# One kernel, three stretches re-ordered: explicit orders in the first mixer, a routing table stored in two parts, and attention woven into the delta recurrence

## The chip, the cores and the metric

The kernel runs on one core of a Trainium2 chip. The number that counts is the device time of one execution in microseconds (us); smaller is better. The core has a matrix engine (TensorE, PE in the profile), a vector engine (DVE), a scalar engine (ACT), a general engine (POOL, used here for indirect loads) and a queue that issues transfers (SP). Each engine executes its own instructions in the order in which they were written for it, and waits at the first one whose inputs are not there.

## The reference

Two layers over 512 tokens of width 1024, in fp32. The first is a mixer (a convolution branch and a linear recurrence) and a layer of 16,384 experts of which each token uses 8 x 16; the second is a hybrid of attention and a gated delta rule.

```
ada = silu(c) @ w_ada + b_ada          # six groups: sh1 sc1 g1 sh2 sc2 g2
z = modulate(rmsnorm(x), sh1, sc1) @ w_in
y_a = gate_b * conv3(gate_c * xa)
y_b = rg_lru(conv4(xr)) * gelu(gr)     # sigmoid gates, exp, sqrt, scan
y = concat(head_rmsnorm(y_a), head_rmsnorm(y_b)) @ w_out
x = x + g1 * y
h = modulate(rmsnorm(x), sh2, sc2)
q = h @ w_q ; sc = q . sub_keys ; top 16 x 16 -> best 16 per head -> softmax g
x = x + g2 * sum_k g_k * gelu(h . U[idx_k]) * V[idx_k]
...
proj = rms_norm(x) @ w_in2             # a_q a_k a_v a_z  d_q d_k d_v d_z  d_b d_a
attn = softmax(a_q a_k^T/8 - slope*dist, causal) @ a_v * silu(a_z)     # 8 heads of 64
o = gated_delta_rule(silu(conv(d_q, d_k, d_v)), g, beta)               # 4 heads of 128, 8 chunks of 64
out = rms_norm(x + rms_norm(concat(attn, rms_norm(o) * silu(d_z)) @ w_out2))
```

With 512 tokens the block selection of the attention takes every earlier block, so it is plain causal attention.

## The kernel before

Activations lie feature-major: 128 partitions by 512 tokens, eight such tiles for the width. An exact fp32 product is made of three fp32r matmuls: `_split` (lines 98 to 103) makes a high part on ACT (line 101: `wH`, `hidH`, `yH`, `cH`, `vH`) and the rest on DVE (line 102: `wL`, `yL`, `vL`), and `_mm3` (lines 106 to 110) adds high x high, high x low and low x high in one PSUM bank. The list scheduler of the framework decides in which order each engine gets the instructions; `tc.issue_after` adds an edge to that order, and the `weave` calls with the numbers of `PLAN` say how generators of work are dealt out against each other.

Five stretches follow one another:

- **First mixer.** `ada(s, dc)` multiplies a 128 x 1024 block of `w_ada` with the broadcast vector `cb` and sums it (line 218, `wada`, DVE). `rms_row` squares (line 265), adds, sums over partitions by tiny matmuls (`ps_ts`), takes the root (line 163 on ACT) and the reciprocal (line 164 on DVE), and spreads it by `ps_row`. Then `xn` (line 298), `hidH` (line 301), and eight steps `dc` of `w_in` into the banks `zp`, `np`, `gp`. The branches end in `headnorm` (lines 386 to 397), and `w_out` runs in two halves of four output tiles on the four `zp` banks, which the update of `xT` on DVE (line 432) releases.
- **Scores, routing, spread.** Top 16 of the scores on DVE (lines 455 to 459), and a dense gate table: one-hot tiles `ohA`, `ohB` (fp16) are multiplied into `ps_g`, 128 x 128 for each token. ACT copies four tokens at a time into `st`, 128 x (128 keys x 32 tokens), and each full `st` (2 MB) goes to `gd` in DRAM (lines 663 and 665).
- **Expert loop.** For each of the 128 first keys `c`: `S = h . U` for 128 experts (`psS`), gelu into `ring`, times the gates `g` read back from `gd` (lines 733 and 741), split into `cH`, `cL`, and `pv` adds `V[c]` (lines 749 to 755).
- **Second mixer.** `proj(m)` is a product of 24 matmuls of 512 columns. `delta_inputs`, `heads` and `recurrence` are the delta rule: inverses of 128 x 128 blocks (`ps_inv`, line 952), transposes (`ps_tm`), then a chain of four steps `ps_w`, `vn`, `ps_s`, `S` (lines 1075 to 1085). `attention(j)` (line 1104) handles two heads of 64 features: the first head's `ps_l` (line 1130, 64 partitions deep) with its softmax, its four value products `ps_ao` (line 1154, 64 columns of weights), and then the second head.
- **Output projection.** `ps_m`, 384 matmuls of 256 columns, whose first bank set is `ps`, `ps`, `ps`, `po`, and the last norms.

Of the kernel before, what the change touches and what calls it, by code (L numbers as in the profile page):

```python
# [20 lines left out]
P = 128  # L21
# [9 lines left out]
GN = 4  # L31
LAG = 46
# [81 lines left out]
PLAN = [(18, 8), (18, 60), (12, 24)]  # L114
# [3 lines left out]
class _Weights:  # L118
# [6 lines left out]
    def get(self):  # L125
        k = self.k
        while self.srcs and len(self.raw) < 2:
            self.load()
        while self.raw and len(self.parts) < 2:
            self.split()  # L130
        return self.parts.pop(0)

# [89 lines left out]
def _phase1(k):  # L222

    nc, tc, I = k.nc, k.tc, k.I
    with tc.tile_pool(name="p1", bufs=1, reuse_waits="tile") as p1, \
# [11 lines left out]
        nc.scalar.activation(out=c1, in_=c1, func=AF.Silu)  # L237
        root = p1.tile([P, 1], F32, name="root")
        nc.scalar.activation(out=root, in_=k.eps, func=AF.Sqrt)
# [22 lines left out]
        def add_square(dc):  # L262
# [4 lines left out]
            if dc:  # L267
                nc.vector.tensor_tensor(out=sqs[0], in0=sqs[0], in1=sq, op=OP.add)

        def rms_row():  # L270

            r = tile_("rms", "rms", 2, (P, 4))
            _rstd(k, r, _token_sums(k, pps, [[sqs[0]]], "np", 2), 1.0 / D)
            sqs.clear()
            return _row_by_transposes(k, pps, lambda tb: r[:, tb:tb + 1].broadcast_to([P, P]), "np", 2)

        for dc in range(KC):
            add_square(dc)
# [5 lines left out]
        rps = rms_row()  # L284
# [5 lines left out]
        for dc in range(KC):  # L290
            sc, sh = ada(1, dc), ada(0, dc)
            nc.vector.tensor_tensor(out=sh, in0=sh, in1=k.col("b_ada", dc, 1), op=OP.add)
            A = A1[:, dc:dc + 1]
            nc.vector.scalar_tensor_tensor(out=A, in0=sc, scalar=k.col("norm1_g", dc, 1), in1=G1[:, dc:dc + 1],
                                           op0=OP.mult, op1=OP.add)
            t = tile_("xn", ("gate0", "gate1")[dc // 4], 4)
            with tc.issue_after(mod.ins) if dc else ExitStack():
                nc.vector.scalar_tensor_tensor(out=t, in0=xT[:, dc, :], scalar=A, in1=row if dc else rps,
                                               op0=OP.mult, op1=OP.mult)
            with tc.issue_after(k.weights.last.ins) if dc else ExitStack():  # L300
                nc.scalar.activation(out=hH[:, dc, :], in_=t, func=AF.Identity, bias=sh)
# [6 lines left out]
        with tc.issue_after(mod.ins):  # L308
            kc_ = _softplus(k, p1, k.neglam, 4, "lru_k")
# [70 lines left out]
        def headnorm(ys, gname, m0):  # L380
# [11 lines left out]
            for j, y in enumerate(ys):  # L392
# [4 lines left out]
                nc.vector.scalar_tensor_tensor(out=y, in0=y, scalar=k.col(gname, j, 1), in1=row,  # L397
                                               op0=OP.mult, op1=OP.mult)
# [17 lines left out]
        g1, sh2, sc2 = (ada_group(s, k.conv_end) for s in (2, 3, 4))  # L416
# [3 lines left out]
        for m in range(KC):  # L420
# [110 lines left out]
def _peer(k, psum):  # L531
# [10 lines left out]
    gd = k.dr.tile([NG, P, NK, GT], F32, name="gd")  # L542
# [25 lines left out]
    with ExitStack() as bctx:  # L568
# [63 lines left out]
        def spread(b, iT, gHL):  # L632
# [11 lines left out]
            for gq in range(P // GT):  # L644
                st = po.tile([P, NK, GT], F32, name="st", tag="st", bufs=2)
                for to in range(0, GT, OG):
# [9 lines left out]
                    for j0 in range(0, OG, 4):  # L656
# [138 lines left out]
def _mixer2(k, psum, pv):  # L795
# [138 lines left out]
    for tb in range(4):  # L934
        for hf in range(2):
# [3 lines left out]
            o = tile_("x3", "lg", 5)  # L939
# [164 lines left out]
    def attention(j):  # L1104
# [13 lines left out]
        nc.scalar.activation(out=az, in_=az, func=AF.Silu)  # L1118
        yield
        po = pps.tile([P, T], F32, name="ps_ao", tag="po", bufs=1)  # L1120
        for hh in range(2):
            h = 2 * j + hh
            off = hh * 64
            rows = slice(off, off + 64)
            slope = 2.0 ** -(h + 1)
            pr = []
            for qb in range(4):
                nk = (qb + 1) * P
# [3 lines left out]
                lg = tile_("lg", "lg", 5)  # L1132
                nc.vector.scalar_tensor_tensor(out=lg[:, 0:nk], in0=C["alibi"][:, 384 - qb * P:512], scalar=slope,
                                               in1=ps[:, 0:nk], op0=OP.mult, op1=OP.add)
                mx = p4.tile([P, 2], F32, name="mx", tag="mx", bufs=6)
                nc.vector.tensor_reduce(out=mx[:, 0:1], in_=lg[:, 0:nk], axis=AX.X, op=OP.max)
                nc.vector.tensor_scalar(out=mx[:, 0:1], in0=mx[:, 0:1], scalar1=-1.0, scalar2=None, op0=OP.mult)
                nc.scalar.activation(out=lg[:, 0:nk], in_=lg[:, 0:nk], func=AF.Exp, bias=mx[:, 0:1],
                                     accum_out=mx[:, 1:2])
                nc.vector.reciprocal(out=mx[:, 1:2], in_=mx[:, 1:2])  # L1140
                nc.vector.tensor_scalar(out=lg[:, 0:nk], in0=lg[:, 0:nk], scalar1=mx[:, 1:2], scalar2=None, op0=OP.mult)
                pr.append(lg)
                yield
            for kb in range(4):
                nq = (4 - kb) * P
                ps = pps.tile([P, T], F32, name="ps_pT", tag="pa", bufs=2)
                for qb in range(kb, 4):
                    nc.tensor.transpose(ps[:, (qb - kb) * P:(qb - kb + 1) * P], pr[qb][:, kb * P:(kb + 1) * P], k.ident)
                pT = tile_("pT", "pT", 3)
                if kb % 2:  # L1150
# [3 lines left out]
                nc.tensor.matmul(out=po[rows, kb * P:T], lhsT=av[:, kb, off:off + 64], rhs=pT[:, 0:nq],  # L1154
                                 start=kb == 0, stop=kb == 3)
                yield
        nc.vector.tensor_tensor(out=az, in0=az, in1=po, op=OP.mult)
        azs.append(az)

# [51 lines left out]
    for _ in A:  # L1211
        pass
    G = chain(gates_of_delta(), gated_norm())
    weave(B, 200, G, 10)
    for _ in G:
        pass
    for az in azs:
        ya = k.px.tile([P, 2, T], F32R, name="ya", tag="row", bufs=4)
        _split(k, az, ya[:, 0, :], ya[:, 1, :])
        yv.append((ya[:, 0, :], ya[:, 1, :]))  # L1220
    yH, yL = k.new_hid()
    for m, y in enumerate(yd):
# [22 lines left out]
    for q in range(4):  # L1245
        acc = [bank("m", tag) for tag in (("ps", "ps", "ps", "po"), ("pp", "pp", "pa", "pa"))[q % 2]]
# [154 lines left out]
```

## Time and profile before

| | before |
|---|---|
| median of 3 runs | 1864.59 us (1864.06 to 1872.85) |
| profiled execution | 1863.24 us, of which span 1861.5 us |
| busy in the span | PE 1777.6 us (95%), DVE 1480.4 (80%), ACT 831.2 (45%), POOL 333.7 (18%) |
| granted TensorE clock, mean | 0.984 |
| first mixer | 0 to 216 us |
| scores, routing, spread | 216 to 566 us |
| expert loop | 566 to 1430 us |
| second mixer, output | 1430 to 1861.5 us |

A span is the time from the first instruction to the last; 1.74 us of the profiled time lie outside it. The shares are means over stretches with different limits, so a stretch has to be read by itself.

### The profile page before, as it was taken

Reading aid. Unit: us, or ns where it says so; the run is one execution under the profiler, and the core shown is the slowest. Engines: PE = TensorE matmul, PEld = TensorE weight load, DVE = VectorE, ACT = ScalarE, POOL = GpSimd, SP = SyncE. Lnnn points to the kernel's source line nnn. Section 1 sums busy time; section 2 is a strip of 40 time slices with the busy share of each in tenths; the row PEclk is TensorE's granted clock in tenths of the full one; section 3 lists DMA queues with packets and bytes.
Section 4 is the critical chain, followed back from the end, with each engine's and each line's share of the span. In section 5 each row is a group of like instructions: output and inputs, shape, how many; then the busy total and the mean of one; then the engine's idle time right before and its main releaser. Section 6 shows DMA issues by size and latency. Waiting matters only on the chain.

```text
span 1861.5 us, 26283 instructions
## 1 busy us (share of the span) xinstructions
PE 1777.6 (95%) x9613; PEld 1542.2 (83%) x9613; DVE 1480.4 (80%) x3012; ACT 831.2 (45%) x1188; POOL 333.7 (18%) x260
## 2 busy tenths in 40 slices
PE   6999898999968999999999999999999999999988
PEld 5777688999957999999999999988887788767768
DVE  7788699999989978888887888898965774566665
ACT  4464534367863433333333333333335753454452
POOL 0000000000000044544444444455400000000000
PEclk9999999999978999999999999999999999999999
DMA  8355333345669789999999999999962311111022
GB/s 307 124 178 208 121 111 108 122 173 215 259 236 284 235 300 372 356 355 331 346 335 342 334 334 349 336 331 345 352 245 76 112 69 58 57 46 46 12 79 91
DMA packets 153414, 404.53 MB, mean 217 GB/s; under 512 B 12098, under 2 KB 64578, under 8 KB 151748
## 3 DMA queue, kind: packets, MB, share of 16 engines
q1 hardware_dynamic: 114690, 243.45, 38.0%
q0 software_dynamic: 36864, 134.23, 19.8%
q10 hardware_dynamic: 1730, 25.17, 3.5%
q8 instruction: 75, 1.23, 0.3%
q14 instruction: 55, 0.45, 0.1%
HBM read 370.30 MB, written 32.51 MB: 216 GB/s over the span
## 4 chain that ended last, share of the span: by engine, by line
PE 84%; DVE 11%; ACT 3%; issue 1%; DMA 1%; DVEq 0%; ACTq 0%; SPq 0%
PE pv L749 10%; PE pv L752 9%; PE pv L755 9%; PE psS L110 8%; PE psS L109 8%; PE psS L108 8%; PE ps_p L109 3%; PE ps_p L108 3%; PE ps_p L110 3%; PE ps_zp L110 2%; PE ps_zp L109 2%; PE ps_zp L108 2%; PE ps_inv L952 2%; DVE wL L102 2%; PE ps_g L660 2%; DVE ohB L640 1%
## 5 line engine op out<-in xcount | busy, mean ns | idle before, releaser
L101 ACT ACTIVATE wH<-wraw 128x1024 fp32r<-128x1024 f32 x204 | 216.4, 1062 | 417.0 <-PE psS L109 257.8
L108 PE MATMUL psS<-hidH,wH 128*128 128x384 f32 x1024 | 346.9, 339 | 3.5 <-ACT ring L554 3.5
L110 PE MATMUL psS<-hidH,wL 128*128 128x384 f32 x1024 | 346.6, 339 | 3.4 <-DVE wL L102 3.4
L109 PE MATMUL psS<-hidL,wH 128*128 128x384 f32 x1024 | 346.6, 338 | 0.0
L102 DVE TENSOR_TENSOR wL<-wraw,wH 128x1024 fp32r<-128x1024 f32 x204 | 248.9, 1221 | 88.7 <-ACT wH L101 88.3
L707 POOL DMA_INDIRECT row<-uN,uidx x128 | 166.4, 1300 | 831.2 <-DVE cL L102 659.0
L749 PE MATMUL pv<-vH,cH 128*128 128x512 f32 x768 | 223.6, 393 | 17.2 <-ACT vH L101 17.2
L755 PE MATMUL pv<-vH,cL 128*128 128x512 f32 x768 | 237.5, 390 | 0.0
L752 PE MATMUL pv<-vL,cH 128*128 128x512 f32 x768 | 237.4, 390 | 0.0
L101 ACT ACTIVATE cH<-ring 128x384 fp32r<-128x384 f32 x128 | 67.2, 526 | 323.0 <-PE pv L752 301.4
L108 PEld LDWEIGHTS psS<-hidH,wH 128*128 128x128 f32 x1024 | 193.4, 189 | 7.7 <-ACT ring L554 4.5
L716 POOL DMA_INDIRECT row<-vR,vidx x128 | 167.1, 1306 | 172.9 <-DVE acc L722 140.8
L110 PEld LDWEIGHTS psS<-hidH,wL 128*128 128x128 f32 x1024 | 193.3, 189 | 5.2 <-DVE wL L102 4.9
L109 PEld LDWEIGHTS psS<-hidL,wH 128*128 128x128 f32 x1024 | 193.3, 189 | 3.2
L749 PEld LDWEIGHTS pv<-vH,cH 128*128 128x128 f32 x768 | 143.7, 189 | 42.3 <-ACT vH L101 17.4
L709 DVE SCALAR_TENSOR_TENSOR row<-row,h2tok 128x1024 f32<-128x1024 f32 x128 | 154.9, 1220 | 25.5 <-DMA row<-uN,uidx 25.4
L722 DVE SCALAR_TENSOR_TENSOR acc<-row,act,acc 128x1024 f32<-128x1024 f32 x127 | 162.6, 1280 | 11.5 <-DMA row<-vR,vidx 10.7
L102 DVE TENSOR_TENSOR vL<-vraw,vH 128x1024 fp32r<-128x1024 f32 x128 | 156.2, 1221 | 18.5 <-ACT vH L101 18.3
L752 PEld LDWEIGHTS pv<-vL,cH 128*128 128x128 f32 x768 | 144.1, 188 | 31.1
L755 PEld LDWEIGHTS pv<-vH,cL 128*128 128x128 f32 x768 | 144.1, 188 | 31.0
L101 ACT ACTIVATE vH<-vraw 128x1024 fp32r<-128x1024 f32 x128 | 135.8, 1061 | 0.4 <-DMA vraw<-vR 0.2
L663 ACT ACTIVATE st<-ps_g 128x512 f32<-128x512 f32 x96 | 96.2, 1145 | 32.3 <-PE ps_g L660 31.7
(415 smaller groups left out, 2973.0 us busy)
## 6 DMA issues: line engine op xcount, KB each, us to landing
wraw<-uT SPq DMA_DIRECT2D x128, 512.0 KB, 5.9
vraw<-vR SPq DMA_DIRECT2D x128, 512.0 KB, 6.6
wraw<-w_in SPq DMA_DIRECT2D x52, 512.0 KB, 3.5
wada<-wada SPq DMA_DIRECT2D x48, 512.0 KB, 4.9
gd<-st ACTq DMA_DIRECT2D x12, 2048.0 KB, 7.3
g<-gd SPq DMA_DIRECT2D x32, 768.0 KB, 9.2
wraw<-w_out SPq DMA_DIRECT2D x16, 512.0 KB, 3.6
wraw<-w_q SPq DMA_DIRECT2D x8, 512.0 KB, 3.5
```

The costliest lines, as they stand in the source:

```text
L101: copy = nc.scalar.activation(out=H, in_=src, func=AF.Copy)
L102: nc.vector.tensor_tensor(out=L, in0=src, in1=H.bitcast(F32), op=OP.subtract)
L108: nc.tensor.matmul(out=ps, lhsT=lH, rhs=rH, start=start, stop=False)
L109: nc.tensor.matmul(out=ps, lhsT=lH, rhs=rL, start=False, stop=False)
L110: nc.tensor.matmul(out=ps, lhsT=lL, rhs=rH, start=False, stop=stop)
L707: nc.gpsimd.indirect_dma_start(out=row, out_offset=None, in_=I["uN"], in_offset=bass.IndirectOffsetOnAxis(ap=uidx[:, n:n + 1], axis=0))
L709: nc.vector.scalar_tensor_tensor(out=row, in0=row, scalar=1.0, in1=h2tok, op0=OP.mult, op1=OP.mult, accum_out=act0[:, n:n + 1])
L716: nc.gpsimd.indirect_dma_start(out=row, out_offset=None, in_=k.vrows, in_offset=bass.IndirectOffsetOnAxis(ap=vidx[:, n:n + 1], axis=0))
L722: nc.vector.scalar_tensor_tensor(out=k.acc0, in0=row, scalar=act0[:, n:n + 1], in1=k.acc0, op0=OP.mult, op1=OP.add)
L749: nc.tensor.matmul(out=pv[b][h], lhsT=cH[:, bs], rhs=vH[:, h * 512:(h + 1) * 512], start=first, stop=False)
L752: nc.tensor.matmul(out=pv[b][h], lhsT=cH[:, bs], rhs=vL[:, h * 512:(h + 1) * 512], start=False, stop=False)
L755: nc.tensor.matmul(out=pv[b][h], lhsT=cL[:, bs], rhs=vH[:, h * 512:(h + 1) * 512], start=False, stop=last)
```

## The change

First mixer: one table of functions less at the start, the loads of the first weights ahead of the modulation blocks, `ada` dealt out one step ahead by explicit edges, the Gelu after the last Sqrt, the `sh2` blocks after `headnorm` of branch a, and the last square of the second norm summed by itself. Spread: `gd` in two DRAM tiles (the first 16 keys, and the other 112), two stores for each `st`, and `st` written so that ACT reads PSUM with a stride and writes four tokens in a row. Second mixer: `softmax(j)` and `values(j)` handle both heads of a pair side by side, the value products of pair j alternate with the projections of pair j + 1, the numbers of `PLAN` differ, and the output projection starts on the banks `pp`, `pp`, `pa`, `pa`.

```diff
+NF = 16
-PLAN = [(18, 8), (18, 60), (12, 24)]
+PLAN = [(18, 8), (18, 56), (12, 32)]
...
+        k.weights.first()
+        with tc.issue_after(added.ins):
+            for s in (1, 0):
+                ada(s, 0)
...
+            if dc < KC - 1:
+                with tc.issue_after(scaled.ins):
+                    for s in (1, 0):
+                        ada(s, dc + 1)
...
-                g = tile_("gg", "gg", 2)
-                nc.scalar.activation(out=g, in_=ps, func=AF.Gelu_apprx_tanh)
+                g = tile_("gg", "gg", 4)
+                with tc.issue_after(gate.ins):
+                    nc.scalar.activation(out=g, in_=ps, func=AF.Gelu_apprx_tanh)
...
-        g1, sh2, sc2 = (ada_group(s, k.conv_end) for s in (2, 3, 4))
+        g1, sc2, sh2 = (ada_group(s, after) for s, after in ((2, k.conv_end), (4, k.conv_end), (3, k.normed)))
...
-    gd = k.dr.tile([NG, P, NK, GT], F32, name="gd")
+    gd = [k.dr.tile([NG, P, n, GT], F32, name="gd%d" % n) for n in (NF, NK - NF)]
...
-                        nc.scalar.activation(out=st[:, :, o:o + 4].rearrange("p n t -> p t n"), in_=ps,
+                        nc.scalar.activation(out=st[:, :, o:o + 4], in_=ps.rearrange("p t n -> p n t"),
                                              func=AF.Copy, scale=1.0 / GSCALE)
-                nc.scalar.dma_start(out=gd[(b - 1) * (P // GT) + gq], in_=st)
+                for part, cs in zip(gd, (slice(0, NF), slice(NF, NK))):
+                    nc.scalar.dma_start(out=part[(b - 1) * (P // GT) + gq], in_=st[:, cs, :])
...
+    def softmax(j, st):
...
+        for qb in range(4):
+            nk = (qb + 1) * P
+            pss = []
+            for rows in halves:
                 ps = pps.tile([P, T], F32, name="ps_l", tag="pa", bufs=2)
                 nc.tensor.matmul(out=ps[:, 0:nk], lhsT=aq[rows, qb * P:(qb + 1) * P], rhs=ak[rows, 0:nk],
                                  start=True, stop=True)
+                pss.append(ps)
...
+            for rows, pT in zip(halves, pts):
+                nc.tensor.matmul(out=po[rows, kb * P:T], lhsT=av[:, kb, rows], rhs=pT[:, 0:nq],
                                  start=kb == 0, stop=kb == 3)
...
+    def attention():
+
+        st = {}
+        yield from projections(0, st)
+        for j in range(4):
+            yield from softmax(j, st)
+            if j < 3:
+                a, b = values(j, st), projections(j + 1, st)
+                for n in range(5):
+                    next(a)
+                    yield
+                    next(b)
+                    yield
...
-    B = chain(delta_inputs(2, ins[1]), delta_inputs(3, ins[1]), *[attention(j) for j in range(4)])
+    B = chain(delta_inputs(2, ins[1]), delta_inputs(3, ins[1]), attention())
...
-        acc = [bank("m", tag) for tag in (("ps", "ps", "ps", "po"), ("pp", "pp", "pa", "pa"))[q % 2]]
+        acc = [bank("m", tag) for tag in (("pp", "pp", "pa", "pa"), ("ps", "ps", "ps", "po"))[q % 2]]
```

The order on ACT where the square roots of the recurrence (`th`, in place) meet the Gelu of its gate (`gg`), before:

```order
L366 ACT_TABLE_LOAD
L366 ACTIVATE th<-th 128x512 x2
L101 ACTIVATE wH<-wraw 128x1024
L405 ACT_TABLE_LOAD
L405 ACTIVATE gg<-ps_zp 128x512
L366 ACT_TABLE_LOAD
L366 ACTIVATE th<-th 128x512 x2
L101 ACTIVATE wH<-wraw 128x1024
L405 ACT_TABLE_LOAD
L405 ACTIVATE gg<-ps_zp 128x512
```

And the same place of the change:

```order
L387 ACT_TABLE_LOAD
L387 ACTIVATE th<-th 128x512 x2
L102 ACTIVATE wH<-wraw 128x1024
L387 ACTIVATE th<-th 128x512
L351 ACTIVATE gcv<-pad,cols 128x512
L387 ACTIVATE th<-th 128x512
L102 ACTIVATE wH<-wraw 128x1024
L351 ACTIVATE gcv<-pad,cols 128x512
L102 ACTIVATE wH<-wraw 128x1024
L427 ACT_TABLE_LOAD
L427 ACTIVATE gg<-ps_zp 128x512
```

Four table loads became two, and no split of a weight (`wH`) stands behind a switch back to the other table any more.

The order on DVE from the root of `headnorm` of branch a (`hnr`) to the first updates of `xT` in `w_out`, before:

```order
L102 TENSOR_TENSOR yL<-xc,yH 128x512 x2
L218 SCALAR_TENSOR_TENSOR wada,ada<-wada,cb 128x1024 x3
L164 RECIPROCAL hnr<-hnr 128x32
L257 TENSOR_TENSOR ada<-ada,cols 128x8
L418 SCALAR_TENSOR_TENSOR A_1245<-ada,cols 128x8
L102 TENSOR_TENSOR wL<-wraw,wH 128x1024
L397 SCALAR_TENSOR_TENSOR gcv<-gcv,cols,ps_row 128x512 x2
L102 TENSOR_TENSOR wL<-wraw,wH 128x1024
L397 SCALAR_TENSOR_TENSOR gcv<-gcv,cols,ps_row 128x512
L102 TENSOR_TENSOR yL<-gcv,yH 128x512
L397 SCALAR_TENSOR_TENSOR gcv<-gcv,cols,ps_row 128x512
L102 TENSOR_TENSOR yL<-gcv,yH 128x512 x3
```

And the same place of the change, up to the updates of `xT` (line 454 there):

```order
L170 RECIPROCAL hnr<-hnr 128x32
L103 TENSOR_TENSOR wL<-wraw,wH 128x1024
L418 SCALAR_TENSOR_TENSOR gcv<-gcv,cols,ps_row 128x512 x2
L103 TENSOR_TENSOR yL<-gcv,yH 128x512
L418 SCALAR_TENSOR_TENSOR gcv<-gcv,cols,ps_row 128x512 x2
L224 SCALAR_TENSOR_TENSOR wada,ada<-wada,cb 128x1024 x3
L103 TENSOR_TENSOR wL<-wraw,wH 128x1024
L103 TENSOR_TENSOR yL<-gcv,yH 128x512 x3
L224 SCALAR_TENSOR_TENSOR wada,ada<-wada,cb 128x1024 x5
L454 SCALAR_TENSOR_TENSOR xT<-ps_zp,ada,xT 128x512 x2
```

The reciprocal has lost the three `wada` ahead of it; eight of them stand now behind it, three ahead of a `wL` and three `yL`, five ahead of the first `xT`.

The order on PE at the last attention pair, where the pairs' products meet the inverses (`ps_inv`, `ps_tm`) of the delta rule, before (the first head's last `ps_ao` and the second head's `ps_l`):

```order
L1154 MATMUL ps_ao<-pT,av 64x256
L1130 MATMUL ps_l<-ak,aq 128x128
L1154 MATMUL ps_ao<-pT,av 64x128
L1130 MATMUL ps_l<-ak,aq 128x256
L959 MATMUL ps_tm<-ca,X 128x128 x4
L952 MATMUL ps_inv<-P_15119,XT 128x128 x4
L1130 MATMUL ps_l<-ak,aq 128x384
L1130 MATMUL ps_l<-ak,aq 128x512
```

And the change at its last pair (x2 are the two heads, at partitions 0 to 63 and 64 to 127):

```order
L1194 MATMUL ps_ao<-pT,av 64x128
L1158 MATMUL ps_l<-ak,aq 128x128
L1194 MATMUL ps_ao<-pT,av 64x128
L1158 MATMUL ps_l<-ak,aq 128x128
L984 MATMUL ps_tm<-ca,X 128x128 x4
L977 MATMUL ps_inv<-X,AM 128x128 x8
L1158 MATMUL ps_l<-ak,aq 128x256 x2
L977 MATMUL ps_inv<-P_15343,XT 128x128 x4
L1158 MATMUL ps_l<-ak,aq 128x384 x2
L984 MATMUL ps_tm<-ca,X 128x128 x4
L977 MATMUL ps_inv<-P_15352,XT 128x128 x4
L1158 MATMUL ps_l<-ak,aq 128x512 x2
```

Where two products 64 deep stood behind one another on the same half of the array, most now stand in pairs on the two halves; the `ps_ao` are mostly still apart.

## Rows read from the trace of the kernel before

**Rows 1.** Busy time by stretch: start:end, length, then each engine's busy us (instructions).

```profile
378.00:500.00 122.00, 122.00 (x1032) 115.03 (x1029) 116.67 (x224) 93.70 (x110) 0.00 (x0) 1.00 0.59 215
500.00:566.00 66.00, 42.51 (x381) 38.11 (x380) 57.55 (x148) 42.04 (x48) 0.00 (x0) 0.78 0.66 250
566.00:1430.00 864.00, 864.00 (x4234) 770.13 (x4234) 717.28 (x1054) 312.55 (x423) 333.51 (x256) 1.00 0.90 318
```

**Rows 2.** Timeline of DVE and PE at the start: start, duration, engine, line, operation [idle before].

```profile
14.81 0.68 DVE L268 TENSOR_TENSOR sq<-sq,sq 128x512 f32<-128x512 f32 x1
...
19.84 1.22 DVE L218 SCALAR_TENSOR_TENSOR wada<-wada,cb 128x1024 f32<-128x1024 f32 x1
...
20.98 0.74 DVE L298 SCALAR_TENSOR_TENSOR xn<-xT,A,ps_row 128x512 f32<-128x512 f32 x1
...
22.54 2.07 PE L108 MATMUL ps_zp<-hidH,wH 128*128 128x512 f32 x4 [3.30 <-ACT hidH L301]
```

**Rows 3.** Timeline of PE around 115 us.

```profile
115.40 0.50 PE L108 MATMUL ps_zp<-hidH,wH 128*128 128x512 f32 x1 [1.53 <-ACT wH L101]
...
117.03 0.58 PE L110 MATMUL ps_zp<-hidH,wL 128*128 128x512 f32 x1 [0.90 <-DVE wL L102]
...
120.39 0.55 PE L109 MATMUL ps_zp<-hidL,wH 128*128 128x512 f32 x1
...
121.94 0.39 PE L109 MATMUL ps_zp<-hidL,wH 128*128 128x512 f32 x1
```

**Rows 4.** Timeline of DVE and PE at the second headnorm.

```profile
165.01 1.23 DVE L218 SCALAR_TENSOR_TENSOR wada<-wada,cb 128x1024 f32<-128x1024 f32 x1 [0.18 <-DMA wada<-wada]
...
168.74 0.35 DVE L164 RECIPROCAL hnr<-hnr 128x32 f32<-128x32 f32 x1
...
176.76 1.89 DVE L102 TENSOR_TENSOR yL<-gcv,yH 128x512 fp32r<-128x512 f32 x3
...
173.28 1.28 PE L182 MATMUL ps_row<-ca,rb 128*128 128x128 f32 x8 [1.56 <-ACT rb L394]
```

**Rows 5.** Groups of ACT: busy us, mean ns of one, idle before.

```profile
L663 ACT ACTIVATE st<-ps_g 128x512 f32<-128x512 f32 x96 | 96.2, 1145 | 32.3 <-PE ps_g L660 31.7 <-ACT st L663 0.5
...
L608 ACT ACTIVATE q<-ps_q 128x512 f32<-128x512 f32 x8 | 4.7, 585 | 0.0
```

**Rows 6.** Timeline from the last tile of the spread to the first `pv`.

```profile
545.81 3.95 ACT L663 ACTIVATE st<-ps_g 128x512 f32<-128x512 f32 x4 [1.71 <-PE ps_g L660]
...
558.17 0.49 DVE L455 MAX8 ts<-s 128x8 f32<-128x128 f32 x2 [4.29 <-DMA s<-sc]
...
563.16 1.50 DVE L741 TENSOR_TENSOR ring<-ring,g 128x384 f32<-128x384 f32 x3 [1.40 <-DMA g<-gd]
...
565.74 1.65 PE L749 MATMUL pv<-vH,cH 128*128 128x512 f32 x3 [17.17 <-ACT vH L101]
```

**Rows 7.** Timeline of PE in the second mixer; fp32 matmuls count twice.

```profile
1748.61 1.12 PE L1130 MATMUL ps_l<-ak,aq 64*128 64x512 f32 x2
1749.67 0.33 PE L1148 MATMUL ps_pT<-ca,lg 128*128 128x128 f32 x1
...
1774.26 1.77 PE L1130 MATMUL ps_l<-ak,aq 64*128 64x384 f32 x4
1775.96 0.66 PE L959 MATMUL ps_tm<-ca,vT 128*128 128x128 f32 x4
```

**Rows 8.** Timeline of PE at the end of the recurrence.

```profile
1783.08 0.44 PE L1148 MATMUL ps_pT<-ca,lg 128*128 128x128 f32 x2 [1.80 <-DVE lg L1141]
...
1789.79 1.06 PE L1075 MATMUL ps_w<-S,nwT 128*128 128x128 f32 x8
...
1794.40 1.06 PE L1075 MATMUL ps_w<-S,nwT 128*128 128x128 f32 x8
...
1810.53 0.28 PE L108 MATMUL ps_m<-wH,hidH 128*128 128x256 f32 x1
```

**Rows 9.** Busy time of ACT on `st` alone, by stretch.

```profile
378.00:500.00 122.00, 63.31 (x63) 1.00 0.59 215
```

More of the change, by code (lines that the diff above doesn't have):

```diff
@@ L131, in get, with first @@
         return self.parts.pop(0)
+    def first(self):
+        self.load()
+        self.split()
     def load(self):
@@ L236, in _phase1 @@
             nc.sync.dma_start(out=xT[:, 2 * q:2 * q + 2, :], in_=I["xT"][:, 2 * q:2 * q + 2, :])
-        nc.scalar.activation(out=c1, in_=c1, func=AF.Silu)
+        silu = nc.scalar.activation(out=c1, in_=c1, func=AF.Silu)
         root = p1.tile([P, 1], F32, name="root")
-        nc.scalar.activation(out=root, in_=k.eps, func=AF.Sqrt)
+        with tc.issue_after(silu.ins):
+            nc.scalar.activation(out=root, in_=k.eps, func=AF.Sqrt)
         nc.scalar.dma_start(out=k.cd, in_=c1)
@@ L290, in _phase1 @@
         for dc in range(KC):
-            sc, sh = ada(1, dc), ada(0, dc)
+            sc, sh = (k.ada[:, s * 8 + dc:s * 8 + dc + 1] for s in (1, 0))
             nc.vector.tensor_tensor(out=sh, in0=sh, in1=k.col("b_ada", dc, 1), op=OP.add)
@@ L1118, in attention @@
         nc.scalar.activation(out=az, in_=az, func=AF.Silu)
+        st[j] = aq, ak, av, az, [[], []]
         yield
[L1120 to L1128, printed above, removed]
+    halves = [slice(0, 64), slice(64, 128)]
+    def softmax(j, st):
+        aq, ak, av, az, pr = st[j]
+        for qb in range(4):
+            nk = (qb + 1) * P
+            pss = []
+            for rows in halves:
                 ps = pps.tile([P, T], F32, name="ps_l", tag="pa", bufs=2)
@@ new lines, in softmax @@
+            for hh, ps in enumerate(pss):
+                lg = tile_("lg", "lg%d" % qb, 2, (P, nk))
+                nc.vector.scalar_tensor_tensor(out=lg, in0=C["alibi"][:, 384 - qb * P:512],
+                                               scalar=2.0 ** -(2 * j + hh + 1), in1=ps[:, 0:nk],
+                                               op0=OP.mult, op1=OP.add)
+                mx = p4.tile([P, 2], F32, name="mx", tag="mx", bufs=10)
+                nc.vector.tensor_reduce(out=mx[:, 0:1], in_=lg, axis=AX.X, op=OP.max)
@@ L1142, in attention, with values @@
-                pr.append(lg)
+                nc.vector.tensor_scalar(out=lg, in0=lg, scalar1=mx[:, 1:2], scalar2=None, op0=OP.mult)
+                pr[hh].append(lg)
                 yield
-            for kb in range(4):
-                nq = (4 - kb) * P
+    def values(j, st):
+        aq, ak, av, az, pr = st[j]
+        po = pps.tile([P, T], F32, name="ps_ao", tag="po", bufs=1)
+        for kb in range(4):
+            nq = (4 - kb) * P
+            pts = []
+            for hh in range(2):
@@ L1207, in _mixer2 @@
     A = chain(heads(ins[0]), heads(ins[1]), recurrence())
-    B = chain(delta_inputs(2, ins[1]), delta_inputs(3, ins[1]), *[attention(j) for j in range(4)])
+    B = chain(delta_inputs(2, ins[1]), delta_inputs(3, ins[1]), attention())
     for na, nb in PLAN:
         weave(A, na, B, nb)
[L1211 to L1220, printed above, removed]
+    for g in (A, B, gated_norm()):
+        for _ in g:
+            pass
     yH, yL = k.new_hid()
-    for m, y in enumerate(yd):
+    for m, y in enumerate(azs + yd):
         _split(k, y, yH[:, m, :], yL[:, m, :])
```

78 lines of the change are left out of this document (46 added, 32 removed).

## The prediction

> **What bounds the kernel now.** I read busy time by stretch first, then the timeline at each place where TensorE (PE) waits, then the groups of ACT. The stretches have different limits. In the expert loop PE is busy for all of its 864 us [rows 1]; the change leaves what PE does there as it was, so these 864 us count as fixed. From 378 to 500 us PE is busy throughout too, with DVE and ACT at 116.7 and 93.7 of 122 us: no engine that gets faster there shortens it by much, and ACT has only 28 us to spare. From 500 to 566 PE is busy for 42.5 of 66 us at a granted clock of 0.78, and DVE for 57.6: that stretch has an end of its own, a chain of DVE work and transfers. What is left to win is in three places: PE's start and its stalls in the first mixer, the 17.2 us without PE before the first `pv` [rows 6], and the second mixer, where PE waits in many small pieces and also does matmuls that use half of its array.
>
> **The change part by part.** All sums are made against the profiled execution, 1863.24 us, which is 1.35 us under the median of the runs.
>
> *Start.* The first matmul waits 3.30 us for `hidH` and begins at 22.54 us [rows 2]. Ahead of it DVE executes `xn` at 20.98, and just before that a `wada` of the next step at 19.84, 1.14 us start to start. The last addition of squares at 14.81 stood behind another `wada` of the same price. With `ada` dealt out by edges the last addition loses its `wada` (1.14), `xn` loses the next step's (1.14), and one split of the next weight, of the same size, goes from in front of `xn` too, while the two `wada` of the first step now stand between the sum and `xn`; part of them lies beside the sums, the root and the row on PE and ACT. The two ends are 1.1 (one of the three) and 3.4 us (all). I take **-2.9**, nearer to all of them: `xn` then starts about when the row is there. Afterwards the eight steps go at PE's pace as before.
>
> *Gelu after Sqrt.* The stall is 1.53 us for `wH` and 0.90 for `wL`, and behind it the matmuls run slower: eight from 117.03 to 120.39, 0.42 us each, against six in 1.55 us from 120.39 to 121.94, 0.26 each [rows 3]. That is 3.36 - 8 x 0.26 = 1.3 us more. Of the four table loads on ACT two go, and no `wH` waits behind them. **-3.7** (ends 0 and -3.7; the first if the weights' split is late for another reason).
>
> *headnorm and w_out.* The reciprocal at 168.74 waited behind three `wada` since 165.01, so PE idled 1.56 us at the row of `rb` [rows 4]. That goes. But eight `wada`, 8 x 1.14 = 9.1 us of DVE, come behind it: three ahead of a `wL` and three `yL` that the first half of `w_out` needs, five ahead of the first `xT`, which frees the bank in which the second half begins. Queued behind them are all later splits, and PE waits for those. Before, DVE had done its last `yL` at 176.76 + 1.89 = 178.65 and was then free until the first half of `w_out` ended. The ends: -1.6 (all nine us lie beside matmuls) and +7.5 (none does). Three `wada` directly ahead of a needed split are hard to hide (3.4 us), five beside some twenty matmuls mostly hidden. 3.4 + 1.2 - 1.6: **+3.0**.
>
> *Spread.* One `st` takes 1145 ns where the copy of `q` from PSUM, of the same size and contiguous on both sides, takes 585 [rows 5]. Before, the write had a stride of 128 bytes; now it writes 16 bytes in a row and the read of PSUM has the stride. No row has a strided read of PSUM. Its bounds are 585 (the write was the cost) and twice 1145 (the read costs more than the write did). I take about 0.8, since a copy without any stride is the nearest form. ACT is not what ends 378 to 500, so a faster `st` gives only its part of the last tile: four in 3.95 us [rows 6], of which 4 x (1.145 - 0.8) = 1.4 us go, less some 0.4 for the second store that ACT now issues: **-1.0**.
>
> The Trainium skill ("SBUF — State Buffer", the note on cachelines) has SBUF in lines of 16 bytes, with a penalty for each access that crosses to a new one, and PSUM in lines of 8 bytes. By it the new write, four fp32 in one line, is the better, and the new read the worse, so it speaks on both sides. The row agrees as far as it goes: the strided write took twice the time. By the rule's PSUM half alone, ACT would gain nothing and the term would be 0.
>
> *Two parts of `gd`.* The first `g` no longer waits for 2 MB, but for 256 KB. PE waits for `vH` and `cH`, `cH` for `ring` at 563.16, which waited 1.40 us for `g` [rows 6]. Ahead of `ring` on DVE stand the searches of the last scores; they waited 4.29 us for `s` until 558.17 and ended when `ring` began to wait, at 561.76. So an earlier `g` alone brings 1.40. More comes only if `s` lands earlier too, and the other 1.75 MB are in flight beside it as before: the end is 4.29 + 1.40 = 5.7. **-1.5**, ends 0 and -5.7.
>
> *Attention in pairs.* A pair of rows prices the matmul: 512 columns took 1749.67 - 1748.61 = 1.06 us, and 384 + 512 columns 1775.96 - 1774.26 = 1.70 [rows 7]. So 384 columns cost 0.64 us, 0.00167 each, and entering and leaving the half array about 0.2. All `ps_l` and `ps_ao` have 2 x 10,240 columns, 34 us. In the order of the change 19 neighbours lie on different halves of the array, before none; the smaller of each two add up to 5,888 columns. If one of a pair runs wholly beside the other, 5,888 x 0.00167 = 9.8 us go. Each fp32 matmul is two passes on the same half, so if matmuls start in order, the second pass of the first must begin before the first pass of the second, and only one pass in four is saved: half of it, 4.9. If the array takes one at a time, 0. I take **-4.9**. The number of switches between whole and half array is 96 in both orders, so nothing comes from that.
>
> The Trainium skill ("TensorE: Matmul & The Clock Gate", Part 3) says that matmuls on different row groups run concurrently, but start and end in order. No row of before has two such neighbours, so nothing in it confirms or denies this. By it alone the term would lie between the two values above.
>
> *Softmax of the last pair.* At 1783.08 PE waits 1.80 us for `lg`, the second head's softmax, in the middle of the recurrence [rows 8]. It now lies before the last projections. **-2.0** with smaller waits of that kind; ends 0 and -4.
>
> *End of the recurrence.* Its steps are 1794.40 - 1789.79 = 4.61 us apart, a chain through DVE, and the last result reaches the projection at 1810.53 [rows 8]. Fifty matmuls of the output projection now fill the first two steps, but they are missing in the last one and in the final norm, where they stood before. **-1.0**, ends +3 and -3.
>
> Sum: first mixer -2.9 - 3.7 + 3.0 = -3.6; spread and transition -2.5; second mixer -7.9. Together -14.0: 1849.2 against the profiled execution, 1850.6 against the median. I say **1850 us**.
>
> **Rivals.** *A, little comes of it (1860):* the halves of the array don't overlap (0) and the `wada` cost their whole price in `w_out` (+7.5 instead of +3.0): -14.0 + 4.9 + 4.5 = -4.6, or 1860. For it speaks that no row shows an overlap; against it that PE has many other waits.
>
> *B, the pairs overlap wholly and `s` lands early (1841):* -4.9 and -4.2 more: -23.1, so 1841. Against it: PE's idle pieces of the second mixer are no shorter for a matmul that ends sooner, where a softmax ends the wait.
>
> *C, the strided read of PSUM makes ACT the bound of the spread (slower):* ACT has 122.0 - 93.7 = 28.3 us to spare for the 63 `st` that lie in 378 to 500 [rows 9], 0.45 us each. From 1.6 us on, each 0.1 us costs 6.3 us there and about 3.4 in the last 34. At twice the price, 2.29 us, that is (1.145 x 63 - 28.3) + 1.145 x 34 = 43.8 + 38.9, less the 24 us in which ACT stands idle in 500 to 566: +59, so about 1910. It turns the sum positive from about 1.75 us for one `st`. For it speaks the strided access; against it that the strided write, which is the only difference to `q` that the rows show, is gone.
>
> *D, the pairs are not pairs:* the scheduler pulled most `ps_ao` apart, so only `ps_l` can gain; that is inside the forecast's half value and A.
>
> **How the numbers follow.** A change of 0.5% is 9.3 us, about what a measurement of this kernel can tell from none. The forecast (-9.3 to -19) has 0.49, B and beyond (more than -19) 0.14, A (between -9.3 and +9.3) 0.28, C 0.09. So faster 0.63, same 0.28, slower 0.09. The range runs from 1837 (B with the small ends) to 1866 (A with the recurrence's +3 and some more); the forecast's own is 1845 to 1855.
>
> **What would show it.** The first `ps_zp` at about 19.6 us; no PE idle near 115; DVE with `wada` between `gcv` and `xT`, and PE idle 2 to 5 us there; a mean of `st` near 0.8 us; the first `pv` 17 us or less after the last `ps_g`, and `ring` ended by a search on DVE, no longer by `g`; two neighbouring `ps_l` of 512 columns in 1.5 us instead of 1.9; no `lg` wait in the recurrence. Wrong it would be by a mean of `st` over 1.6, by neighbours that take their full price one after another, or by PE waits in the second mixer that the new order of softmax and projections brings and that no row of before can show.

## The result and the profile after

The change takes 1842.45 us (median of 4 runs, 1840.83 to 1845.23); the kernel before, measured again beside it, 1867.34 (1864.06 to 1872.85). The ratio is 0.9865, with a 95% interval of 0.9835 to 0.9895: faster by 1.35%. The profiled executions are 1863.24 and 1840.83 us, with spans of 1861.5 and 1839.1, both at a mean granted clock of 0.984: 22.4 us less, where the prediction's sum was 14.0.

The same events in both traces say where it went (us from the start of the span):

| | before | change | difference | predicted, summed up |
|---|---|---|---|---|
| first `ps_zp` | 22.54 | 19.46 | -3.08 | -2.9 |
| first matmul of `w_out` | 157.72 | 150.04 | -7.68 | -6.6 |
| last matmul of `w_out` | 208.17 | 206.20 | -1.97 | -3.6 |
| first `ps_q` (end of the first mixer) | 215.66 | 212.33 | -3.33 | -3.6 |
| first `ps_t` (routing) | 336.27 | 335.75 | -0.52 | -3.6 |
| last `ps_g` | 548.26 | 546.89 | -1.37 | -4.6 |
| first `pv` | 565.74 | 563.17 | -2.57 | -6.1 |
| last `pv` | 1429.60 | 1426.08 | -3.52 | -6.1 |
| first `ps_w` (recurrence) | 1780.45 | 1766.60 | -13.85 | |
| last `ps_m` | 1853.61 | 1830.92 | -22.69 | |
| end of span | 1861.48 | 1839.06 | -22.42 | -14.0 |

The second mixer, from the last `pv` to the end, went from 431.9 to 413.0 us, 18.9 less instead of 7.9. All the rest together gave 3.5.

The timeline of the change at its start, DVE and PE, answers to [rows 2]:

```profile
15.84 0.08 DVE L224 DVE_READ_ACCUMULATOR wada<-wada,cb 128x1 f32 x1
...
17.24 0.08 DVE L224 DVE_READ_ACCUMULATOR wada<-wada,cb 128x1 f32 x1
17.91 0.75 DVE L314 SCALAR_TENSOR_TENSOR xn<-xT,A,ps_row 128x512 f32<-128x512 f32 x1 [0.40 <-ACT rrow L301]
...
19.46 2.08 PE L109 MATMUL ps_zp<-hidH,wH 128*128 128x512 f32 x4 [2.22 <-ACT hidH L321]
```

Both `wada` of the first step (blocks of the modulation weights) end before `xn`, and `xn` waits 0.40 us for the row: it starts when the row is there, as the step said.

The timeline of PE around 105 us and at `w_out`, and of DVE between, answers to [rows 3, 4]:

```profile
105.13 0.50 PE L111 MATMUL ps_zp<-hidH,wL 128*128 128x512 f32 x1 [0.67 <-DVE wL L103]
...
168.38 1.22 DVE L224 SCALAR_TENSOR_TENSOR wada<-wada,cb 128x1024 f32<-128x1024 f32 x1
169.52 0.08 DVE L224 DVE_READ_ACCUMULATOR wada<-wada,cb 128x1 f32 x1
169.52 1.22 DVE L103 TENSOR_TENSOR wL<-wraw,wH 128x1024 fp32r<-128x1024 f32 x1
...
178.23 1.23 DVE L224 SCALAR_TENSOR_TENSOR wada<-wada,cb 128x1024 f32<-128x1024 f32 x1 [2.00 <-DMA wada<-wada]
...
170.80 0.80 PE L111 MATMUL ps_zp<-yH,wL 128*128 128x512 f32 x1 [3.21 <-DVE wL L103]
171.39 0.63 PE L109 MATMUL ps_zp<-yH,wH 128*128 128x512 f32 x1
...
181.54 0.47 PE L109 MATMUL ps_zp<-yH,wH 128*128 128x512 f32 x1 [0.72 <-DVE xT L454]
...
183.68 0.50 PE L109 MATMUL ps_zp<-yH,wH 128*128 128x512 f32 x1 [0.84 <-ACT wH L102]
```

Of the 2.43 us of waits at the Gelu 0.67 are left, and no slow matmuls follow. At `w_out` PE waits 3.21 us for the split that stands behind three `wada`, and then matmuls take 0.63 us in the records instead of 0.39: the granted clock is at the lower of its two levels, 1.2 GHz, and it falls again behind the waits of 0.72 and 0.84, some 7 us in all. Of the last five `wada`, the fourth waits 2.00 us for its own load, and `xT` with it.

The groups of ACT in the change, answering to [rows 5], and its timeline before the first `pv`, answering to [rows 6]:

```profile
L686 ACT ACTIVATE st<-ps_g 128x512 f32<-128x512 f32 x96 | 52.3, 597 | 53.3 <-PE ps_g L683 49.3 <-issue 2.6 <-ACT st L686 0.5
...
L631 ACT ACTIVATE q<-ps_q 128x512 f32<-128x512 f32 x8 | 4.7, 584 | 0.0
```

```profile
557.09 0.49 DVE L477 MAX8 ts<-s 128x8 f32<-128x128 f32 x2 [4.55 <-DMA s<-sc]
...
560.40 0.28 DVE L478 MATCH_REPLACE8 work<-ts,s 128x128 f32<-128x128 f32 x1
560.60 1.49 DVE L766 TENSOR_TENSOR ring<-ring,g 128x384 f32<-128x384 f32 x3
...
563.17 2.93 PE L774 MATMUL pv<-vH,cH 128*128 128x512 f32 x6 [15.96 <-ACT vH L102]
```

One `st` takes 597 ns, 13 more than the contiguous copy of `q`; more than that the strided read doesn't cost. `ring` follows the last search without a wait, so `g` no longer ends it; `s` still lands late (4.55 us), and PE waits 15.96 instead of 17.17.

And PE in the second mixer, answering to [rows 7]:

```profile
1643.55 1.13 PE L1158 MATMUL ps_l<-ak,aq 64*128 64x512 f32 x4
1644.61 0.50 PE L110 MATMUL ps_p<-hidL,wH 128*128 128x512 f32 x1
...
1708.24 1.07 PE L1194 MATMUL ps_ao<-pT,av 128*64 128x512 f32 x2
1709.24 0.55 PE L1184 MATMUL ps_pT<-ca,lg 128*128 128x128 f32 x3
```

This is the line that the forecast missed. Two `ps_l` of 512 columns (x4, since each counts twice) take 1644.61 - 1643.55 = 1.06 us. Before, one took 1.06. The pair costs what one costs. (The trace has the first passes of the two halves start at 1643.55 and 1643.56 us and the second ones at 1644.08 and 1644.09, so the passes alternate between the halves.) Below it is a `ps_ao` whose partner was pulled away: alone it still takes 1.00.

### The profile page after: what moved, and what is told of

Read it like the earlier page. It is cut to its first block, busy times and chain, and to the rows that moved or that the text cites. A ratio compares the mean times of both kernels' runs of the same rounds, so it can differ in the third digit from the quotient of the medians.

```text
span 1839.1 us, 26310 instructions
## 1 busy us (share of the span) xinstructions
PE 1765.5 (96%) x9621; PEld 1536.9 (84%) x9621; DVE 1481.8 (81%) x3013; ACT 781.4 (42%) x1182; POOL 332.6 (18%) x260
## 4 chain that ended last, share of the span: by engine, by line
PE 83%; DVE 11%; ACT 3%; issue 1%; DMA 1%; ACTq 0%; SPq 0%; DVEq 0%
PE pv L774 10%; PE pv L777 10%; PE pv L780 10%; PE psS L111 9%; PE psS L109 9%; PE psS L110 9%; PE ps_p L109 3%; PE ps_p L110 3%; PE ps_p L111 3%; PE ps_inv L977 2%; PE ps_zp L109 2%; PE ps_zp L111 2%; PE ps_zp L110 2%; PE ps_g L683 2%; DVE wL L103 2%; PE ps_ao L1194 1%
## 5 line engine op out<-in xcount | busy, mean ns | idle before, releaser
L103 DVE TENSOR_TENSOR cL<-ring,cH 128x384 fp32r<-128x384 f32 x128 | 71.0, 556 | 56.3 <-ACT cH L102 56.0
```

What stands on the lines that cost most here:

```text
L103: nc.vector.tensor_tensor(out=L, in0=src, in1=H.bitcast(F32), op=OP.subtract)
```

## The experiments

The lengths of the second mixer, from the last `pv` to the end of the span, and the start of the first `ps_q`, are read from each run's trace; the ratio is against the kernel before, run on the same chip.

| | ratio (95%) | first `ps_q` | second mixer | estimate at clock 0.984 |
|---|---|---|---|---|
| before | | 215.7 | 431.9 | 1863.3 |
| the change | 0.9865 (0.9835 to 0.9895) | 212.3 | 413.0 | 1840.5 |
| e1, second mixer alone | 0.9893 (0.9872 to 0.9915) | 215.5 | 412.9 | 1844.2 |
| e2, `st` alone | 1.0005 (0.9989 to 1.0022) | 215.3 | 435.9 | 1862.9 |
| e3, two parts of `gd` alone | 0.9992 (0.9972 to 1.0012) | 214.1 | 434.4 | 1862.3 |
| e4, first mixer alone | 1.0011 (0.9994 to 1.0027) | 211.3 | 438.6 | 1862.2 |
| e5, pairs apart | 0.9877 (0.9841 to 0.9913) | 211.5 | 421.6 | 1844.0 |
| e6, old output banks | 0.9864 (0.9828 to 0.9901) | 210.2 | 417.8 | 1841.1 |
| e7, all pairs | 0.9839 (0.9809 to 0.9870) | 210.0 | 415.2 | 1836.8 |
| e8, all pairs, `sh2` late | 0.9804 (0.9777 to 0.9832) | 205.6 | 413.1 | 1831.3 |
| e9, no alternation | 0.9901 (0.9876 to 0.9925) | 211.2 | 419.0 | 1844.7 |
| e10, `sh2` late | 0.9843 (0.9821 to 0.9864) | 205.7 | 416.3 | 1835.0 |

The kernel before ran between 1861 and 1878 us in these comparisons, and stretches that two kernels share differ by 2 to 7 us between traces (the second mixers of e2, e3 and e4 are that of before). Most of this goes with the granted clock. The mean clock of a run lies between 0.974 and 0.985, and within each kernel, over the 108 runs that have it on record, 0.001 of it is worth 1.26 us; about that line only 1.2 us (standard deviation) are left. The last column is an estimate from it: the mean of a kernel's runs, taken along the line to 0.984, with a standard error of 0.2 to 1.2 us. It also takes out whatever an edit itself does to the clock.

So the length of a stretch says little until the clock is taken out of it. For the second mixer the traces allow that. The matmuls of attention that use half of the array can be summed by themselves (rows of a window over the whole span; busy us and instructions of PE, of its weight loads, of DVE). Before, `ps_l` and then `ps_ao`:

```profile
0.00:1900.00 1900.00, 23.59 (x64) 9.90 (x64) 15.32 (x32) 0.98 0.60 213
0.00:1900.00 1900.00, 22.16 (x64) 6.86 (x64) 2.73 (x4) 0.98 0.60 213
```

The change:

```profile
0.00:1900.00 1900.00, 14.81 (x64) 5.65 (x64) 14.59 (x32) 0.98 0.60 213
0.00:1900.00 1900.00, 20.67 (x64) 5.19 (x64) 2.74 (x4) 0.98 0.60 213
```

And e5, in which the pairs are pulled apart:

```profile
0.00:1900.00 1900.00, 19.69 (x64) 7.80 (x64) 14.74 (x32) 0.98 0.61 213
0.00:1900.00 1900.00, 22.15 (x64) 6.34 (x64) 2.73 (x4) 0.98 0.61 213
```

With PE's idle time and its other matmuls, which are the same in number in every run, the second mixer divides like this (us; the last column is the time in it at the clock's lower level):

| | length | `ps_l`, `ps_ao` | PE idle | other matmuls | at 1.2 GHz |
|---|---|---|---|---|---|
| before | 431.9 | 45.8 | 24.1 | 362.0 | 10.2 |
| the change | 413.0 | 35.5 | 19.2 | 358.3 | 6.1 |
| e1 | 412.9 | 35.5 | 17.9 | 359.5 | 11.7 |
| e5 | 421.6 | 41.8 | 17.4 | 362.4 | 18.2 |
| e6 | 417.8 | 35.2 | 19.4 | 363.2 | 17.6 |
| e7 | 415.2 | 29.2 | 19.4 | 366.6 | 21.9 |
| e8 | 413.1 | 29.2 | 18.9 | 365.0 | 19.3 |
| e9 | 419.0 | 38.7 | 19.2 | 361.1 | 12.2 |
| e10 | 416.3 | 35.5 | 17.6 | 363.2 | 19.5 |

No `ps_l` or `ps_ao` ran at the lower level in these traces, so the column of the pairs is free of the clock. The column of the other matmuls follows it: at 1.2 GHz those of `w_out` started 0.43 us apart instead of 0.23, so up to half of such time is lost. e10 has the second mixer's code of the change and 13.4 us more at 1.2 GHz, so differences of this size come without any edit in it.

**One part at a time.** e1 has only the edits of the second mixer, e2 only the two lines of `st`, e3 only the two DRAM tiles with `st` written as before, e4 only the edits ahead of `gd`.

```diff
# e2
-  nc.scalar.activation(out=st[:, :, o:o + 4].rearrange("p n t -> p t n"), in_=ps,
+  nc.scalar.activation(out=st[:, :, o:o + 4], in_=ps.rearrange("p t n -> p n t"),
# e3
-  gd = k.dr.tile([NG, P, NK, GT], F32, name="gd")
+  gd = [k.dr.tile([NG, P, n, GT], F32, name="gd%d" % n) for n in (NF, NK - NF)]
```

> The kernel before with only the second mixer of the change. In the profile of the change the stretch from the last pv to the end is 413.0 us against 431.9 before, 18.9 less. Theory: this comes from the second mixer's own order (pairs on two halves of the array, and fewer waits), so it stands alone: a span 17 to 20 us under that of before, neighbouring ps_l of 512 columns in 1.07 us. Rival: it needs the earlier stretches (loads of weights that come earlier); then 8 to 12 us.

> The kernel before with only the eviction of ps_g changed (strided read of PSUM, four tokens in a row written). Theory: one st takes 0.60 us instead of 1.145, but ACT doesn't end these stretches, so the last ps_g comes 0.5 to 1.5 us earlier and the time is 1 to 2 us less. Rival: ACT was the hidden bound of the spread; then the 0.55 us times 96 show in part, 5 us or more.

> The kernel before with only the gate table in two DRAM tiles and two stores for each st. Theory: the first g lands earlier, and the searches on DVE end the wait of ring instead: the wait of PE before the first pv falls from 17.17 us by 1 to 1.5. Rival: the searches wait for s just as long and the second store on ACT costs as much as the first gains; 0 or slightly slower.

> The kernel before with only the first mixer of the change. In the profile of the change the first ps_q came 3.3 us earlier, and the first ps_t 0.5 us, since PE ran at the low clock a little longer at two places in between. Theory: that giving back belongs to the earlier part itself, so here too about 0.5 to 1 us is left at the end of the kernel. Rival: it is another part of the change that gave it back; then 3 us are left.

e1 took 1843.73 us, and its second mixer is as short as that of the whole change, 412.9 us: the theory holds, the gain stands alone. By the estimate at one clock the four parts bring 19.1 (e1), 0.4, 1.0 and 1.1 us, together 21.6 of the change's 22.8.

e2: one `st` takes 596 ns (group below), the stretch from the first `ps_t` to the last `ps_g` falls from 212.0 to 210.9 us, and the time doesn't move; the expected 1 to 2 us lie inside its interval.

```profile
L663 ACT ACTIVATE st<-ps_g 128x512 f32<-128x512 f32 x96 | 52.2, 596 | 50.6 <-PE ps_g L660 49.8
```

Of the 44 us of work that ACT lost, 18 came back at this place as waits for `ps_g` (31.7 us before, 49.8 now). e3: from the last `ps_g` to the first `pv` 16.6 us instead of 17.5, 0.9 where 1 to 1.5 was expected; too little for a median.

e4: the first `ps_q` came at 211.3 us, 4.3 earlier, the first `ps_t` at 334.9, only 1.4 earlier, the first `pv` at 564.2, 1.5 earlier, and the median is no shorter. Its second mixer took 6.7 us more than that of before, which is the same code in a slightly different order of the scheduler, with 27.4 us at 1.2 GHz instead of 10.2. The theory that the first mixer's own gain is what is given back does not stand: e5, e6, e7 and e9 have the instructions of the change in the same order up to the first `ps_t`, and there it came at 332.6, 333.8, 333.7 and 332.1 us, 2.4 to 4.1 earlier than before. How much is given back differs from one execution to the next, with the clock.

**Pairs apart, and all pairs.** e5 deals the halves out 0 0 1 1, e7 lets one release make both ready.

```diff
# e5, in softmax and likewise in values
+        for hh, qb in ((0, 0), (0, 1), (1, 0), (1, 1), (0, 2), (0, 3), (1, 2), (1, 3)):
# e7, in softmax; in values both copies of pT stand on one engine, h1's first
+            pss = [pps.tile([P, T], F32, name="ps_l", tag="pa", bufs=2) for hh in range(2)]
...
+            one = logits(0)            # into pss[1], which comes free last
+            with tc.issue_after(one.ins):
+                logits(1)              # into pss[0]
```

> The change with softmax and values dealing the two halves in the order 0 0 1 1 instead of 0 1 0 1, each matmul right behind its own input: neighbours on different halves of the array have 1,920 columns in common instead of 5,888. Theory: the overlap of such neighbours is the main part of the gain of the second mixer; 3,968 columns at 0.00167 us are 6.6 us, so about 1849. Rival: the gain comes from where softmax and values stand among the projections, not from the pairs; then 1842 to 1844.

> The change with both halves of a pair made ready by the same release: the matmul whose bank comes free last is issued first, the other behind it by an edge, and both copies of pT on one engine. Neighbours on different halves now have 8,960 columns in common, and 83 switches of the array's form remain of 96. Theory: 3,072 more columns are 5.1 us, and 13 switches at 0.14 another 1.8, so 1835 to 1838. Rival: the halves now wait for each other, and PE loses in waits what it gains; 1842 or more.

e5: PE is busy with `ps_l` and `ps_ao` for 6.4 us more, where the overlap theory had 6.6 and the rival 0. The second mixer takes 8.6 us more, but with 12.1 us more at 1.2 GHz and 1.8 us less of PE's waits (each matmul now stands right behind its own input), so the length alone would not have decided. The median, 1845.79, is 3.3 above that of the change, and the estimates at one clock differ by 3.5: the overlap is shown, and part of what it costs to undo it comes back as shorter waits.

e7: PE's time on `ps_l` and `ps_ao` falls by another 6.3 us, close to the 6.9 of the theory, and PE's idle time stays the same, 19.4 against 19.2. So the rival, that the halves lose in waits what they gain, does not hold. The second mixer is 2.2 us longer all the same, since the other matmuls take 8.3 us more, with 15.8 us more at 1.2 GHz. The timeline of e7 in the recurrence has the waits for `vn` and for `u_all` that the change has (printed below):

```profile
1778.32 1.16 PE L1108 MATMUL ps_s<-vn,ik 128*128 128x128 f32 x8 [0.78 <-DVE vn L1103]
...
1788.11 0.55 PE L1254 MATMUL ps_oT<-ca,u_all 128*128 128x128 f32 x3 [2.10 <-DVE u_all L1124]
```

The median gains 2.0 us, inside the interval. At one clock the estimate is 3.7 us, and 3.7 again from e10 to e8, which differ by the same edit: about half of the expected 7. Where the other 2 to 3 us of PE's time stay isn't shown.

**Output banks, and no alternation.** e6 swaps the two sets of banks back; e9 lets `values(j)` end before `projections(j + 1)` begins.

> The change with the old first banks of the output projection (ps, ps, ps, po), so that it can't begin before the recurrence is done with them. Theory: the fifty matmuls that now stand in the first two steps of the recurrence, 5.9 us, filled time in which PE would wait; 3 to 6 us slower, 1845 to 1848. Rival: the chain of the recurrence and of the last norm sets that end in both; within 1 us of the change.

> The change with the values of a pair first and the projections of the next pair after them, instead of dealt out alternately; all else as in the change. Neighbours on different halves keep 4,480 of 5,888 columns (2.4 us more) and 109 switches stand for 96 (1.8 us more). Theory: beside the pairs, dealing projections between the value products takes PE's small waits away; then the second mixer, from the last pv to the end, takes 8 to 10 us more than the 413.0 of the change. Rival: the alternation itself brings nothing; then 4 us more, about 417.

e6: from the first `ps_w` to the last `ps_m` 68.7 us instead of 64.3. That looks like the expected 3 to 6 us, but 27 `ps_m`, 3.2 us, stand ahead of the first `ps_w` in the change, and none in e6, so most of the 4.4 is work that crossed the mark. PE's idle time in this stretch is 0.9 us longer (three waits of 0.78 us for `vn` instead of one, less a later wait of 0.67), in the whole second mixer 0.2; the 4.8 us by which that is longer are other matmuls, with 11.5 us more at 1.2 GHz. The median, 1843.92, is 1.5 above the change and the estimate at one clock 0.6. So the rival holds: the banks bring about a microsecond at most. The timeline of the recurrence in the change, which answers to [rows 8], has the early `ps_m` and what is left of the waits:

```profile
1760.95 0.39 PE L109 MATMUL ps_m<-wH,hidH 128*128 128x256 f32 x1
...
1766.60 0.83 PE L1100 MATMUL ps_w<-S,nwT 128*128 128x128 f32 x6
...
1779.52 1.16 PE L1108 MATMUL ps_s<-vn,ik 128*128 128x128 f32 x8 [0.78 <-DVE vn L1103]
...
1789.31 0.55 PE L1243 MATMUL ps_oT<-ca,u_all 128*128 128x128 f32 x3 [2.10 <-DVE u_all L1124]
1790.48 0.66 PE L1243 MATMUL ps_oT<-ca,u_all 128*128 128x128 f32 x4 [0.63 <-DVE dz L1245]
```

The wait of 1.80 us for `lg` is gone, and the last norm's waits, 2.10 + 0.63, stand where 1.48 and 0.62 stood. e9: 6.0 us more, 419.0, between the theory (8 to 10) and the rival (4). Of these, 3.3 are `ps_l` and `ps_ao` (fewer pairs and more switches, 4.2 expected) and 2.8 other matmuls, with 6.1 us more at 1.2 GHz; PE's idle time is the same, 19.2. So the alternation takes none of PE's waits away, and the rival holds; the estimate at one clock is 4.2 us more, near its 4.

**`sh2` late.** The waits at `w_out` were the one price in the trace of the change that an edge can take away.

```diff
-        g1, sc2, sh2 = (ada_group(s, after) for s, after in ((2, k.conv_end), (4, k.conv_end), (3, k.normed)))
+        g1, sc2 = (ada_group(s, k.conv_end) for s in (2, 4))
...
+            if m == 3:
+                sh2 = ada_group(3, upd)    # upd: the update of xT above
```

> As the run with all pairs, and the eight blocks of sh2 issued after the fourth update of xT instead of after headnorm. In the change PE waits 3.2 us for a split behind three of them, 0.7 and 0.8 at the second half of w_out, and runs at the low clock for about 7 us after these waits. Theory: 4.8 us of waits and 3 us of low clock go, so the first ps_q comes 5 to 8 us earlier, and 2 to 5 us remain at the end: about 1832. Rival: the next stretches give it back, as they did with the 3.3 us of the first mixer: as the run with all pairs alone.

> The change with only the eight blocks of sh2 issued after the fourth update of xT. Theory: the waits of 3.2, 0.7 and 0.8 us at w_out go, with the low clock behind them; the first ps_q comes 4.5 to 7 us before the 212.3 of the change, and all of it remains, 1835 to 1838 us. Rival: in the run with all pairs and late sh2 it was the pairs that brought the 8 us; then 1840 or more.

e10 took 1837.29 us and e8 1831.76. In both the first `ps_q` comes at 205.7 us, 6.6 before that of the change, as expected, and it remains: the last `pv` starts 6.5 us earlier in e10 and 8.4 in e8, and at one clock e10 is 5.5 us under the change. In the timeline of e10 one wait of 0.55 us is left in `w_out` where three stood:

```profile
177.35 0.50 PE L111 MATMUL ps_zp<-yH,wL 128*128 128x512 f32 x1 [0.55 <-DVE wL L103]
```

e8 is the fastest version found, 2% under the kernel before.

## Why the prediction held, and where it was off

The sign and the range held, for reasons that were partly the stated ones; the 22.4 us of the profile are half as much again as the 14.0 of the sum, and lie in B's place rather than the forecast's. That is in part luck, since only one of B's two conditions came true: the pairs overlap wholly, but `s` landed no earlier.

- *Start, -2.9:* -3.08, by the named step.
- *Gelu, -3.7:* 0.67 us of wait is left, and no low clock behind it. From the first `ps_zp` to the first matmul of `w_out` 4.6 us went, 0.9 more than the sum had.
- *headnorm and `w_out`, +3.0:* from the first to the last matmul of `w_out` it is +5.7. The waits are 3.21 + 0.72 + 0.84 us, close to the price of the `wada` (3.4 + 1.2), but the low clock after them was not in the sum. e10 prices the place: 6.6 us come back when the `wada` leave it. Behind `w_out` 1.4 us went that no term had, where the last square is summed by itself. The first mixer's sum is right (-3.33 for -3.6) because these differences cancel.
- *What was not in the sum:* 2.8 of these 3.3 us were gone at the first `ps_t`. Busy time in 324 to 329 us, with the granted clock as the third number from the end, in the change:

```profile
324.00:329.00 5.00, 5.00 (x20) 5.00 (x21) 5.00 (x16) 0.00 (x0) 0.00 (x0) 0.66 0.42 146
```

  And before:

```profile
324.00:329.00 5.00, 3.51 (x19) 3.19 (x20) 5.00 (x14) 0.65 (x2) 0.00 (x0) 1.00 0.29 100
```

  The granted clock was 0.66 there, so most of it at the lower of its two levels, 1.2 GHz; before it was 1.00. PE had waited 1.00 and 0.78 us just ahead of it, as it had before. PE's matmuls of 384 columns started 0.32 us apart instead of 0.17, and `psS` lost 1.6 us. Another 1.2 us went in the same way at the start of `ps_q`. The sum takes for granted that the gain of a stretch is kept. In this execution it wasn't; in e5, e6, e7 and e9, with the same instructions up to there, 2.4 to 4.1 us were left at the first `ps_t`, around the 3.6 of the sum. Why the clock fell in one execution and not in another isn't settled.
- *`st`, -1.0:* -0.85 between `ps_t` and the last `ps_g`. The duration, 597 ns instead of 0.8 us, is the low end of the bounds; that it hardly matters was right.
- *Two parts of `gd`, -1.5:* -1.20, with the search as what is late next, as said.
- *Attention in pairs, -4.9:* this is the term that was mis-sized. The sum took one pass in four as saved, because two passes on one half were thought to stand one after another before the other half's could begin. The trace shows the pair in the time of one, the passes alternating between the halves: PE's time on these matmuls fell by 10.3 us, the full bound of 9.8, and undoing 3,968 of the 5,888 columns (e5) brought 6.4 of it back. The Trainium skill ("TensorE: Matmul & The Clock Gate", Part 3) models such a pair as the time of one matmul and a few ns; the row agrees with that.
- *Softmax of the last pair and end of the recurrence, -2.0 and -1.0:* the `lg` wait went. The output matmuls in the recurrence are worth 1 us at most by e6, about as summed. In all PE's idle time in the second mixer fell by 4.9 us where the sum had 3.0. The largest wait that went and was in no term is one of 2.48 us of a `ps_p` for `aq`, at 1675.65 us before; neither the banks (e6) nor the alternation (e9) changes the total.
- *The rest of the 18.9 us:* 3.7 us are other matmuls, which had no term. With 4.1 us less at 1.2 GHz in this execution, about 2 of them are the clock; the other 2 aren't told apart.

## What to carry to other kernels

Matmuls that use half of the array's rows or columns cost half only when they stand next to a partner on the other half, so look at the order that the scheduler made, and not at the source: of 32 possible pairs here 19 came out as neighbours. A gain can be gone 100 us later in one execution and be there in the next of the same instructions; read it at several events and in several traces. Before a length is put down to an edit, look at the granted clock, and sum the edited instructions and the engine's idle time by themselves: here the lengths of e6, e7 and e9 each pointed at a wrong cause. Work that is moved off one chain (the `wada` ahead of a reciprocal) must be followed to where it lands: here it came to stand ahead of a weight split, and moving it once more was worth more than the rest of the first mixer's edits.

## What the runs showed of the hardware

Reading PSUM with a stride of 512 bytes on ACT and writing 16 bytes in a row took 597 ns for 128 x 512, against 585 for a contiguous copy and 1145 for a contiguous read with writes 128 bytes apart: the write's stride was all but 12 ns of the cost. The Trainium skill's note on cachelines ("SBUF — State Buffer") fits on the side of SBUF; its warning of strided PSUM access, given there for matmuls, doesn't show on this read. Two fp32 matmuls on the two halves of the array ran in the time of one, 1.06 us for 512 columns. And the granted clock fell at different places in different executions of shared code: the same second mixer had 6.1 us at 1.2 GHz in one trace and 19.5 in another, and over 108 runs 0.001 of the mean clock went with 1.26 us of the time.
